# A weight sum of the attention branch worked out ahead and fetched, and one more seven-product quad in its first pass

## The chip, the cores and the metric

The kernel runs on one core of one Trainium2 chip. The metric is the device time of one execution in microseconds (us). Three runs of the kernel before gave a median of 1379.91 us (1379.5 to 1380.3).

## The reference, cut to what matters

One layer of a hybrid block on 256 rows of width 2048: a normalised input is projected (`proj`), one part goes through dilated attention, one through a state-space scan, and both come back through a gated sum:

```python
proj = hn @ w_in
q, k, v, z_a, z_s, xbc, dt_raw, g_a, g_s = jnp.split(proj, split_points, axis=-1)
...
o_a = o_a.reshape(b, s, ATTN_WIDTH) * jax.nn.silu(z_a)
...
merged = jax.nn.sigmoid(g_a) * (o_a @ w_attn_branch) + jax.nn.sigmoid(g_s) * (y @ w_ssm_branch)
return x + merged @ w_out
```

The change is about `o_a @ w_attn_branch`: 256 x 2048 times 2048 x 2048, in fp32.

## The kernel before, in words

**Products in three matmuls.** The matrix engine (PE) takes fp32r operands, so each fp32 operand is split into a high part (`h`, a copy by ACT) and a low part (`l = w - h`, a subtraction by DVE). A product is the triple h·h, h·l, l·h (`triple`, L484 to L486): three 128x512 matmuls. A PE instruction for `l` thus stands behind a DMA, an ACT copy and a DVE subtraction.

**Units, quads and passes.** Weights come as units of 128x1024 floats (512 KB) over SP's DMA queue, in an order laid out on the host. The GEMMs `ssm`, `v`, `ga`, `attn` and `out` run in two passes, c = 0 and c = 2, each of two column blocks of 512. A pass goes over its k in quads (two k-tiles, both row halves, both column blocks) in a written order (`A_ORDERS` for attn). A plain quad is 8 triples, 24 matmuls, and two units. A quad named in `S_QUADS` is done with seven products as in Strassen's method: 21 matmuls, for which it needs the weights A11 and A12 (tile `wa`, one unit), B22 (`wc`, half a unit), T (`wt`, one unit, a sum of weight blocks) and U = `wa` minus T's second half. On the side of the activations it needs `sx`, sums of activation blocks. In attn the first pass has the seven-product quads 2, 4, 6, the second 2, 4, 5, 6.

**Where T and U come from.** The sums T of ga, attn and out are worked out while the PE projects q, k and za (in the profile, some 825 to 1116 us): every 3.75 weight units a job of `sum_jobs` loads a unit and half a unit into `th_a` (L250, with a small POOL copy ahead that orders it behind unit u), three units later DVE makes T with two subtractions (L254, L255) and SP spills it to DRAM (L242). In the attn pass T is fetched into a place in `fin` (L533), B22 into another (L534), and U is made in place on DVE from `wa` (L565), at which point `la` has read `wa` already.

**Two banks of sums, a fold, two seams.** The seven products go to PSUM in two sets: `ps` tiles (results) and `pp` tiles (four products that several results share). At the end of a pass `fold` (L587 to L594) adds the four `pp` tiles up: two ACT copies, then DVE L591 (third `pp` tile), L592 (fourth), L593, L594; after that `ps` and fold are added (L1154) and merged with the gate (`merge`, L1143, L1144). In the first pass these run at the program's own priority, in the second ahead of it (`M_AHEAD`). Weight splits run 120 places ahead (`L_AHEAD`). Where one pass ends and the next begins (the seam), DVE has to serve both: the fold of the old pass and the low parts of the new one. All engines and the SP queue take their instructions in program order; that order is set by a scheduler from the written order and these priorities. Units are numbered through; 433 to 448 are those of attn's second pass (`l433` is the low part of its first unit, `ltt437` that of T of its first seven-product quad). `mtp` are 128x128 transposes on the PE of the merged rows (L1136).

Of the kernel before, what the change touches and what calls it, by code (L numbers as in the profile page):

```python
# [9 lines left out]
F32 = mybir.dt.float32  # L10
# [5 lines left out]
P = 128  # L16
# [8 lines left out]
UNIT = 1024  # L25
# [12 lines left out]
GT_LAGS = (3, 5, 6), (2, 3, 4)  # L38
Y_AFTER = 0, 0
GS_BEFORE = {0: (0, 1), 4: (2,)}  # L40
A_ORDERS = {0: (0, 1, 2, 4, 3, 6, 5, 7), 2: (0, 2, 1, 4, 3, 5, 6, 7)}
V_ORDERS = {0: (0, 2, 4, 1, 3, 5, 6, 7), 2: (0, 2, 1, 4, 3, 5, 6, 7)}
G_ORDERS = {c: (0, 2, 4, 1, 3, 5, 6, 7) for c in (0, 2)}
O_LEFT = {0: {0: (0, 3), 4: (1, 5)}, 2: {}}
# [5 lines left out]
S_QUADS = {  # L50
    ("ssm", 0): (5, 7, 8, 10, 11, 12, 13), ("ssm", 2): (3, 5, 7, 8, 10, 11, 12, 13),
    ("v", 0): (2, 3, 4, 5, 6), ("v", 2): (2, 4, 5, 6), ("ga", 0): (2, 3, 4, 5, 6), ("ga", 2): (2, 3, 4, 5, 6),
    ("attn", 0): (2, 4, 6), ("attn", 2): (2, 4, 5, 6), ("out", 0): (3, 5), ("out", 2): (3, 5),
}
Y_ORDERS = {0: (0, 1, 2, 3, 5, 4, 7, 8, 6, 10, 11, 9, 12, 14, 13, 15), 2: (0, 3, 1, 5, 2, 7, 8, 4, 10, 11, 6, 12, 9, 13, 14, 15)}
Y_LATE = {12: 4, 13: 6}
SX_Y = sorted({*S_QUADS[("ssm", 0)], *S_QUADS[("ssm", 2)]}, key=Y_ORDERS[0].index)
Y_SPARE = {q: int(q in S_QUADS[("ssm", 0)] and q in S_QUADS[("ssm", 2)]) for q in SX_Y}
SX_X = (2, 4, 3, 5, 6)
O_BEHIND = 3, 14, 15, 17  # L60
SUMS_ATT = [(t, q) for t in [(n, c) for n in ("ga", "attn", "out") for c in (0, 2)] for q in S_QUADS[t]]
ATT_QUADS = sorted({*S_QUADS[("attn", 0)], *S_QUADS[("attn", 2)]})
IN_PLACE = {"ssm": [(0, 12), (2, 12)]}
SUMS_SSM = [(t, q) for t in (("ssm", 0), ("ssm", 2), ("v", 0), ("v", 2)) for q in S_QUADS[t] if (t[1], q) not in IN_PLACE.get(t[0], ())]
# [134 lines left out]
def hybrid_block(ctx: ExitStack, tc: tile.TileContext, wall, xt, x, pk_d, cst_d, fw_d, out):  # L199
# [28 lines left out]

    loaded = {}
    on_unit = {}  # L230
    presum, lefts = {}, {}
    ssm_pool = []

    def behind_unit(n, f):
        on_unit.setdefault(n, []).append(f)
# [5 lines left out]
        kept[key] = dram.tile([P, *shape], F32, name=name, tag=name)  # L241
        nc.sync.dma_start(kept[key], src)  # L242

    def sum_jobs(jobs, units, places):

        def get(tag, q, t, b11, behind):
            n = FIRST[tag] + 2 * q
            for dst, src in ((t, wall[n + 1]), (b11, wall[n, :, :512])):
                gp.tensor_copy(dst[:, 0:1], behind)
                nc.sync.dma_start(dst, src)  # L250

        def add(tag, q, t, b11, res, behind):
            gp.tensor_copy(res[:, 0:1], behind)
            ve.tensor_tensor(res[:, :512], t[:, :512], b11, ALU.subtract)  # L254
            ve.tensor_tensor(res[:, 512:], t[:, 512:], res[:, :512], ALU.subtract)  # L255
            spill(presum, (tag, q), f"t_{tag[0]}{tag[1]}_{q}", res, [UNIT])

        for n, ((tag, q), u) in enumerate(zip(jobs, units)):
            t, b11, res = places[n % len(places)]
            behind_unit(u, lambda behind, a=(tag, q, t, b11): get(*a, behind))  # L260
            behind_unit(u + SUM_LAG, lambda behind, a=(tag, q, t, b11, res): add(*a, behind))

    def load(n, cuts=(0, UNIT)):
        if n not in loaded:
# [204 lines left out]
    def gemm_pair(tag, x_of, n_kt, sxs, swap, extra={}, close=1, order=None, room={}, tail=None):  # L469
# [22 lines left out]
        for at, q in enumerate(order):  # L492
            tick()
            for f in extra.get(q, ()):
                f()
            ks = [x_of(2 * q + k) for k in range(2)]
            a = [[(x[:, i * P : (i + 1) * P], x[:, S + i * P : S + (i + 1) * P]) for x in ks] for i in range(2)]
            n = first + 2 * q
            if q not in quads:
                ready = [] if at <= n_q - close else ready  # L500
                ready += [(a, k, *unit(n + k, (2, 512))) for k in range(2)]
                if n_q - close <= at < n_q - 1:
                    continue
                steps = [(e, i, c) for e in ready for i in range(2) for c in range(2)]
                if at == n_q - 1:
                    steps.sort(key=lambda s: s[1:])
                jobs = [(e, i, c, es[2 * i + c], WHOLE, at == 0 and e[1] == 0, e is ready[-1]) for e, i, c in steps]
                if tail and at == n_q - 1:
                    es.append(tail(prods))
                    _, i, c = steps[-1]  # L510
                    jobs = jobs[:-3]
                    for acc, cs in ((es[3][:, LEFT], LEFT), (es[4][:, LEFT], RIGHT)):
                        for n, e in enumerate(ready[-3:]):
                            jobs.append((e, i, c, acc, cs, cs is RIGHT and n == 0, n == 2))
                for (ae, k, h, l), i, c, acc, cs, start, stop in jobs:
                    triple(acc, *ae[i][k], h[:, c, cs], l[:, c, cs], start=start, stop=stop and at == n_q - 1)
                continue
            if not prods:
                prods = banks(p_tags, "pp")
            made = (tag, q) in presum  # L520

            def place(kind):
                if not room.get(kind):
                    t = ring(f"{kind}{n}")
                    return t[:, 512:] if kind == "wc" else t
                seats[kind] = seats.get(kind, -1) + 1
                return room[kind][seats[kind] % len(room[kind])]

            wa = ring(f"wa{n}")
            nc.sync.dma_start(wa, wall[n])  # L530
            if made:
                wt, wc = place("wt"), place("wc")
                nc.sync.dma_start(wt, presum[tag, q])  # L533
                nc.sync.dma_start(wc, wall[n + 1, :, 512:])  # L534
            else:
                wt = ring(f"wb{n}")
                wc = wt[:, 512:]
                nc.sync.dma_start(wt, wall[n + 1])

            def hl(where, suffix, tags, bufs):  # L540
                return [
                    where.tile([P, UNIT], F32R, name=f"{t}{suffix}{n}", tag=t, bufs=bufs) for t in tags
                ]

            def pair_of(suffix):
                sets = room.get("tl", ())
                seats["tl"] = (seats.get("tl", -1) + 1) % (2 + len(sets))
                return sets[seats["tl"] - 2] if seats["tl"] > 1 else hl(mul, suffix, ("ht", "lt"), 2)

            def part(src, h, l):  # L550
                ac.activation(h, src, AF.Copy)  # L551
                ve.tensor_tensor(l, src, h.bitcast(F32), ALU.subtract)  # L552

            two = lambda t: t.rearrange("p (k m) -> p k m", k=2)
            with tc.high_priority(L_AHEAD):
                if not made:
                    ve.tensor_tensor(wt[:, :512], wt[:, :512], wa[:, :512], ALU.subtract)
                ha, la = hl(stream, "a", "hl", H_BUFS)
                part(wa, ha, la)
                hc, lc = hl(stream, "c", "hl", H_BUFS)  # L560
                part(wc, hc[:, :512], lc[:, :512])
                if not made:
                    ve.tensor_tensor(wt[:, 512:], wt[:, 512:], wt[:, :512], ALU.subtract)
                t2 = wt[:, 512:].unsqueeze(1).to_broadcast([P, 2, 512])
                ve.tensor_tensor(two(wa), two(wa), t2, ALU.subtract)  # L565
                ht, lt = pair_of("t")
                part(wt, ht, lt)
                hu, lu = pair_of("u")
                part(wa, hu, lu)
            sx = sxs[q]  # L570
            lo, hi = slice(0, 512), slice(512, 1024)
            go, end = q == seven[0], q == seven[-1]
            for acc, x, h, l, cs, own in (
                (prods[0], a[0][0], ha, la, lo, True),
                (es[0], a[0][1], ha, la, hi, False),
                (es[1], sx[3], hc, lc, lo, False),
                (prods[1], sx[0], ht, lt, lo, True),
                (prods[2], sx[2], ht, lt, hi, True),
                (prods[3], sx[1], hu, lu, lo, True),
                (es[2], a[1][1], hu, lu, hi, False),  # L580
            ):
                triple(acc, *x, h[:, cs], l[:, cs], start=(own and go), stop=(own and end))
# [109 lines left out]
    with tc.tile_pool(name="ssm", bufs=2) as sp:  # L692
# [212 lines left out]
        for c in GS_BEFORE[0]:  # L905
# [4 lines left out]
        begin = FIRST[("xs", 4)]  # L910
        sum_jobs(
            SUMS_SSM, [FIRST[("B", g)] + n for g in range(1, 7) for n in SUM_UNITS],
            [(sums_at[:, 0], sums_at[:, 2, :512], sums_at[:, 1])],
        )

        def left_x(q, behind):
# [127 lines left out]
    with tc.tile_pool(name="att", bufs=2) as ap:  # L1044
# [33 lines left out]
        def mix(h, pT, za):  # L1078
# [10 lines left out]
            if h % 2 == 1 and q in ATT_QUADS:  # L1089
# [1 line left out]

        sum_jobs(
            SUMS_ATT, [FIRST[("q", 0)] + 3 + n * 15 // 4 for n in range(len(SUMS_ATT))],
            [
                (th_a[:, i, :UNIT], th_a[:, 1, UNIT + 512 * i : UNIT + 512 * i + 512], th_a[:, 0, UNIT:])
                for i in range(2)
            ],
        )

        for h in range(NH):  # L1100
# [23 lines left out]
            open_gate(c, es, prods)  # L1124
        tick(final=True)

    with tc.tile_pool(name="fin", bufs=2) as fp:
        fin = big.tile([P, 2, D], F32, name="fin", tag="yo1a")
        room = {"wt": [fin[:, i, UNIT:] for i in range(2)], "wc": [fin[:, i, :512] for i in range(2)]}

        def turn_m(c, pair, b):
            tp = bank(b, 4 if b == "g" else 2, f"mtp{c}{pair}")
# [26 lines left out]
        for n in range(4):  # L1159
            after(T_LAGS[n // 2], lambda a=(n // 2, n % 2, "g"): turn_m(*a))  # L1160
        attend(2)
        for n in range(4):
            after(M_LAG + 1 + n // 2, lambda a=(2 + n // 2, n % 2, ("m1", "m2")[n % 2]): turn_m(*a))
        for n in range(4):
# [118 lines left out]
```

## Time and profile before

| what | value |
|---|---|
| median of 3 runs | 1379.91 us (1379.5 to 1380.3) |
| profiled execution, its own time | 1379.87 us |
| its span, first to last instruction | 1378.0 us |
| around the span | 1.87 us |
| mean granted clock of the PE | 0.998 |

The profile is one execution. Busy time of an engine leaves out its waits; DMA share is the mean busy share of the core's 16 DMA engines, and GB/s is what they moved. On the profile's clock the stages are: up to 745 us the state-space branch, 745 to 825 v, 825 to 1116 q, k, za with the attention heads, 1116 to 1200 ga, 1200 to 1284 attn, then out.

### The profile page before, as it was taken

What the parts mean: (1) busy time and instruction counts of PE and PEld (TensorE: products, weight loads), DVE (VectorE), ACT (ScalarE), POOL (GpSimd) and SP (SyncE); (2) the same over time, 40 slices, a digit from 0 to 9 for tenths busy, and PEclk for the clock granted to TensorE, in tenths of its full rate; (3) what the DMA queues carried; (4) which work ended last, traced back from release to release, by engine and by line L of the source; (5) the groups of instructions that cost most, each with busy time, mean ns of one, the idle gap of its engine ahead of it and who ended that gap; (6) DMA issues with size and microseconds to landing.
All of it is one profiled execution on the core that took longest, in us unless ns stands there. A gap on an engine that the chain in (4) does not pass through costs nothing.

```text
span 1378.0 us, 20734 instructions
## 1 busy us (share of the span) xinstructions
PE 1366.8 (99%) x7260; PEld 1164.8 (85%) x7260; DVE 1177.0 (85%) x1763; ACT 840.0 (61%) x1310; POOL 161.7 (12%) x238
## 2 busy tenths in 40 slices
PE   9999999999999999999999999999999999999997
PEld 7888888888888888888888888888888888888886
DVE  6898899898899888788989888777877789988897
ACT  7655777675667676666565554454444557655564
POOL 2301211101020100010001001211211000400112
PEclk9999999999999999999999999999999999999999
DMA  9767878778787867578677568888889757875773
GB/s 342 237 190 237 298 267 286 262 244 288 248 277 237 298 203 220 174 242 277 228 261 270 211 215 316 306 275 280 306 298 302 230 163 267 291 244 173 246 273 122
DMA packets 106520, 348.15 MB, mean 253 GB/s; under 512 B 11888, under 2 KB 14256, under 8 KB 106416
## 3 DMA queue, kind: packets, MB, share of 16 engines
q1 hardware_dynamic: 104400, 340.67, 74.0%
q10 hardware_dynamic: 1440, 4.06, 0.8%
q0 software_dynamic: 576, 2.10, 0.4%
q8 instruction: 57, 0.93, 0.3%
q14 instruction: 47, 0.39, 0.1%
HBM read 316.97 MB, written 29.82 MB: 252 GB/s over the span
## 4 chain that ended last, share of the span: by engine, by line
PE 98%; DMA 0%; DVE 0%; ACT 0%; issue 0%; SPq 0%; POOL 0%; POOLq 0%; DVEq 0%
PE ps_xs L333 8%; PE ps_zs L333 8%; PE ps_k L333 4%; PE ps_za L333 4%; PE ps_q L333 4%; PE ps_zs L339 4%; PE ps_xs L339 4%; PE ps_ssm L485 3%; PE ps_ssm L486 3%; PE ps_ssm L484 3%; PE ps_q L339 2%; PE ps_za L339 2%; PE ps_k L339 2%; PE ps_gs L421 2%; PE ps_gs L422 2%; PE ps_gs L420 2%
## 5 line engine op out<-in xcount | busy, mean ns | idle before, releaser
L278 ACT ACTIVATE h<-w 128x1024 fp32r<-128x1024 f32 (+1 forms) x394 | 410.0, 1048 | 306.0 <-issue 73.7
L279 DVE TENSOR_TENSOR l<-w,h 128x1024 fp32r<-128x1024 f32 (+1 forms) x394 | 474.0, 1209 | 111.1 <-ACT h L278 106.9
L333 PE MATMUL ps_zs<-XT,h 128*128 128x512 f32 x496 | 172.0, 393 | 0.0
L333 PE MATMUL ps_xs<-XT,h 128*128 128x512 f32 x496 | 171.6, 393 | 0.0
L339 PE MATMUL ps_zs<-XT,l 128*128 128x256 f32 x496 | 134.6, 279 | 0.0
L339 PE MATMUL ps_xs<-XT,l 128*128 128x256 f32 x496 | 133.7, 277 | 0.0
L333 PEld LDWEIGHTS ps_xs<-XT,h 128*128 128x128 f32 x496 | 91.3, 188 | 19.4
L333 PEld LDWEIGHTS ps_zs<-XT,h 128*128 128x128 f32 x496 | 91.3, 188 | 18.9
L339 PEld LDWEIGHTS ps_zs<-XT,l 128*128 128x128 f32 x496 | 93.3, 188 | 2.1
L339 PEld LDWEIGHTS ps_xs<-XT,l 128*128 128x128 f32 x496 | 93.2, 188 | 2.1
L333 PE MATMUL ps_q<-XT,h 128*128 128x512 f32 x256 | 91.1, 404 | 0.0
L333 PE MATMUL ps_k<-XT,h 128*128 128x512 f32 x256 | 88.6, 395 | 0.0
L333 PE MATMUL ps_za<-XT,h 128*128 128x512 f32 x256 | 88.4, 394 | 0.0
L551 ACT ACTIVATE ha<-wa 128x1024 fp32r<-128x1024 f32 x45 | 47.5, 1056 | 45.9 <-PE ps_ssm L486 10.0
L339 PE MATMUL ps_q<-XT,l 128*128 128x256 f32 x256 | 68.4, 278 | 0.0
L339 PE MATMUL ps_k<-XT,l 128*128 128x256 f32 x256 | 68.4, 277 | 0.0
L339 PE MATMUL ps_za<-XT,l 128*128 128x256 f32 x256 | 68.4, 277 | 0.0
L552 DVE TENSOR_TENSOR la<-wa,ha 128x1024 fp32r<-128x1024 f32 x45 | 54.8, 1218 | 8.4 <-ACT ha L551 8.3
L552 DVE TENSOR_TENSOR ltu<-wa,htu 128x1024 fp32r<-128x1024 f32 x40 | 48.7, 1219 | 10.8 <-ACT htu L551 10.8
L793 ACT ACTIVATE gt<-acb,acT 128x128 f32<-128x128 f32 x128 | 44.1, 390 | 22.2 <-DMA acb<-acum_d 21.9
L333 PEld LDWEIGHTS ps_k<-XT,h 128*128 128x128 f32 x256 | 47.0, 188 | 9.9
L333 PEld LDWEIGHTS ps_q<-XT,h 128*128 128x128 f32 x256 | 47.1, 188 | 9.7
(691 smaller groups left out, 3347.8 us busy)
## 6 DMA issues: line engine op xcount, KB each, us to landing
w<-in_wall SPq DMA_DIRECT2D x390, 512.0 KB, 4.8
wa<-in_wall SPq DMA_DIRECT2D x45, 512.0 KB, 4.7
th_a<-in_wall SPq DMA_DIRECT2D x21, 512.0 KB, 4.7
sums_at<-in_wall SPq DMA_DIRECT2D x18, 512.0 KB, 5.0
acb<-acum_d SPq DMA_DIRECT2D x32, 256.0 KB, 3.8
t_ssm<-sums_at SPq DMA_DIRECT2D x13, 512.0 KB, 4.3
wt<-t_ssm SPq DMA_DIRECT2D x13, 512.0 KB, 4.7
th_a<-in_wall SPq DMA_DIRECT2D x21, 256.0 KB, 5.4
```

The source lines that it names most:

```text
L278: ac.activation(h[:, a:b], w[:, a:b], AF.Copy)
L279: ve.tensor_tensor(l[:, a:b], w[:, a:b], h[:, a:b].bitcast(F32), ALU.subtract)
L333: high = pe.matmul(acc, h[:, kk, :], xs_of(kt), start=(kt == 0), stop=False)
L339: low = pe.matmul(acc[:, S:], l[:, kk, :], xs_of(kt)[:, :S], start=False, stop=(kt == KT - 1))
L420: pe.matmul(accs[i], xh, h[:, kk], start=(kt == 0), stop=False)
L421: pe.matmul(accs[i], xh, l[:, kk], start=False, stop=False)
L484: pe.matmul(acc, xh, h, start=start, stop=False)
L485: pe.matmul(acc, xh, l, start=False, stop=False)
L486: pe.matmul(acc, xl, h, start=False, stop=stop)
L551: ac.activation(h, src, AF.Copy)
L552: ve.tensor_tensor(l, src, h.bitcast(F32), ALU.subtract)
L793: ac.activation(g4[:, n, b], acb[:, j, b // 2 * P : b // 2 * P + P], AF.Relu, scale=-1.0, bias=sc[:, h : h + 1],)
```

## The change

Three things change, all in the attention branch.

1. Quad 5 of attn's first pass becomes a seven-product quad (its `sx` is there already, the second pass uses it), and the order of the first pass becomes 0, 1, 2, 4, 5, 6, 3, 7, so four seven-product quads stand in a row and two plain quads at the end.
2. U of all eight seven-product quads of attn is worked out in `sum_jobs`, behind T. Such a job loads a whole unit in place of half a one, has one more DVE subtraction of 128x1024 (L264) and one more spill of 512 KB to DRAM. T's result goes to a tile of the pool `mul` (tag `lt`, two buffers) in place of a part of `th_a`. There are 22 jobs in place of 21.
3. In the attn passes U is fetched (L550) like T, into a new pool `branch` (tile `room_a`) with two places for U and two for B22, which no longer goes into `fin`. The DVE subtraction that made U in place (now L579) stays for the other GEMMs, and runs no more in attn.

```diff
-A_ORDERS = {0: (0, 1, 2, 4, 3, 6, 5, 7), 2: (0, 2, 1, 4, 3, 5, 6, 7)}
+A_ORDERS = {0: (0, 1, 2, 4, 5, 6, 3, 7), 2: (0, 2, 1, 4, 3, 5, 6, 7)}
...
-    ("attn", 0): (2, 4, 6), ("attn", 2): (2, 4, 5, 6), ("out", 0): (3, 5), ("out", 2): (3, 5),
+    ("attn", 0): (2, 4, 5, 6), ("attn", 2): (2, 4, 5, 6), ("out", 0): (3, 5), ("out", 2): (3, 5),
...
+U_QUADS = 2, 4, 5, 6
+SUMS_U = {(t, q) for t, q in SUMS_ATT if t[0] == "attn" and q in U_QUADS}
...
-            for dst, src in ((t, wall[n + 1]), (b11, wall[n, :, :512])):
+            b = b if (tag, q) in SUMS_U else b[:, :512]
+            for dst, src in ((t, wall[n + 1]), (b, wall[n, :, : b.shape[-1]])):
...
+            if (tag, q) in SUMS_U:
+                t2 = res[:, 512:].unsqueeze(1).to_broadcast([P, 2, 512])
+                two = b.rearrange("p (k m) -> p k m", k=2)
+                ve.tensor_tensor(two, two, t2, ALU.subtract)
+                spill(u_sums, (tag, q), f"u_{tag[0]}{tag[1]}_{q}", b, [UNIT])
...
+            if (tag, q) in u_sums:
+                wu = place("wu")
+                nc.sync.dma_start(wu, u_sums[tag, q])
...
-                t2 = wt[:, 512:].unsqueeze(1).to_broadcast([P, 2, 512])
-                ve.tensor_tensor(two(wa), two(wa), t2, ALU.subtract)
+                if (tag, q) not in u_sums:
+                    wu = wa
+                    t2 = wt[:, 512:].unsqueeze(1).to_broadcast([P, 2, 512])
+                    ve.tensor_tensor(two(wa), two(wa), t2, ALU.subtract)
...
-                part(wa, hu, lu)
+                part(wu, hu, lu)
...
-        room = {"wt": [fin[:, i, UNIT:] for i in range(2)], "wc": [fin[:, i, :512] for i in range(2)]}
+        spots = bp.tile([P, 3 * UNIT], F32, name="room_a", tag="room_a")
+        room = {
+            "wt": [fin[:, i, UNIT:] for i in range(2)],
+            "wu": [spots[:, i * UNIT : (i + 1) * UNIT] for i in range(2)],
+            "wc": [spots[:, 2 * UNIT + i * 512 : 2 * UNIT + i * 512 + 512] for i in range(2)],
+        }
```

How the order of instructions moves is shown at two places. Names carry a running number at their end; a name such as `pp_attn0_2` is the third `pp` tile of the first pass, `ps_attn2_0` the first result tile of the second. Lines of the kernel after are its own: L288 is L279 of before, L493 to L495 are L484 to L486, L564 is L552, L605 to L608 are L591 to L594, L1160, L1161 and L1171 are L1143, L1144 and L1154, L1153 is L1136.

**The seam between the two attn passes, on DVE.** Before, from the first fold step on:

```order
L591 TENSOR_TENSOR fin_12298<-pp_attn0_2_12380,fin_12298 128x512
L279 TENSOR_TENSOR l432_12589<-w432_12586,h432_12588 128x1024
L552 TENSOR_TENSOR ltt437_12721<-fin_12298,htt437_12720 128x1024
L592 TENSOR_TENSOR fin_12298<-pp_attn0_3_12381,fin_12298 128x512
L593 TENSOR_TENSOR fin_12298<-fin_12298 128x512
L279 TENSOR_TENSOR l433_12670<-w433_12667,h433_12669 128x1024
L594 TENSOR_TENSOR fin_12298<-fin_12298 128x512
L279 TENSOR_TENSOR l434_12676<-w434_12673,h434_12675 128x1024
L1154 TENSOR_TENSOR fin_12298<-ps_attn0_0_12299,fin_12298 128x512
```

And in the changed kernel, from the same step on:

```order
L605 TENSOR_TENSOR fin_12353<-pp_attn0_2_12436,fin_12353 128x512
L1171 TENSOR_TENSOR fin_12353<-ps_attn0_0_12355,fin_12353 128x512
L564 TENSOR_TENSOR ltt437_12783<-fin_12353,htt437_12782 128x1024
L1160 SCALAR_TENSOR_TENSOR th_a_7802<-th_a_7802,fin_12353 128x512
L606 TENSOR_TENSOR fin_12353<-pp_attn0_3_12437,fin_12353 128x512
L1161 SCALAR_TENSOR_TENSOR th_s_90<-th_a_7802,th_s_90 128x512
L607 TENSOR_TENSOR fin_12353<-fin_12353 128x512
L564 TENSOR_TENSOR ltu437_12787<-room_a_12354,htu437_12786 128x1024
L608 TENSOR_TENSOR fin_12353<-fin_12353 128x512
L1171 TENSOR_TENSOR fin_12353<-ps_attn0_1_12356,fin_12353 128x512
L288 TENSOR_TENSOR l433_12732<-w433_12729,h433_12731 128x1024
L288 TENSOR_TENSOR l434_12738<-w434_12735,h434_12737 128x1024
```

Before, five instructions stand between the first fold step's start and `l433`; in the changed kernel ten do (L605 counted in both cases).

**The same seam on PE.** Before, the second pass begins with `h433`, and `l433` is its second matmul:

```order
L486 MATMUL ps_attn0_3_12302<-h432_12588,oaTb_10585 128x512
L484 MATMUL ps_attn2_0_12635<-h433_12669,oaTa_8484 128x512
L485 MATMUL ps_attn2_0_12635<-l433_12670,oaTa_8484 128x512
L486 MATMUL ps_attn2_0_12635<-h433_12669,oaTa_8484 128x512
L484 MATMUL ps_attn2_1_12636<-h433_12669,oaTa_8484 128x512
```

In the changed kernel, first the last matmul into the third `pp` tile, then, 26 matmuls on, the seam:

```order
L495 MATMUL pp_attn0_2_12436<-htt429_12577,sx_o6_12371 128x512
...
L495 MATMUL ps_attn0_2_12357<-h432_12650,oaTb_10619 128x512
L1153 MATMUL mtp00_12701<-cst_77,th_s_90 128x128
L493 MATMUL ps_attn2_0_12697<-h433_12731,oaTa_8484 128x512
L493 MATMUL ps_attn2_1_12698<-h433_12731,oaTa_8484 128x512
L493 MATMUL ps_attn2_2_12699<-h433_12731,oaTa_8484 128x512
L493 MATMUL ps_attn2_3_12700<-h433_12731,oaTa_8484 128x512
L1153 MATMUL mtp01_12708<-cst_77,th_s_90 128x128
L494 MATMUL ps_attn2_0_12697<-l433_12732,oaTa_8484 128x512
```

Between the last matmul into `pp_attn0_2` and the first with `l433` stand 31 matmuls of 128x512 and two transposes. Two transposes of the first pass's rows (`mtp00`, `mtp01`) now stand ahead of `l433`; their PSUM banks are those of `ps_attn0_0` and `ps_attn0_1`, which L1171 has to have read.

**The SP queue in the second pass of ga.** Here the attn branch's first fetches stand among the loads of ga's weights. Before:

```order
L533 DMA fin_12298<-t_attn0_2_9856 128x1024
L534 DMA fin_12298<-in_wall 128x512
L533 DMA fin_12298<-t_attn0_4_9965 128x1024
L534 DMA fin_12298<-in_wall 128x512
L267 DMA w404_12076<-in_wall 128x1024
L533 DMA th_a_7802<-t_ga2_3_9358 128x1024
L530 DMA wa407_12109<-in_wall 128x1024
```

In the changed kernel:

```order
L542 DMA fin_12353<-t_attn0_2_9867 128x1024
L542 DMA fin_12353<-t_attn0_4_9980 128x1024
L276 DMA w404_12131<-in_wall 128x1024
L542 DMA th_a_7802<-t_ga2_3_9365 128x1024
L543 DMA room_a_12354<-in_wall 128x512
L550 DMA room_a_12354<-u_attn0_2_9870 128x1024
L543 DMA room_a_12354<-in_wall 128x512
L550 DMA room_a_12354<-u_attn0_4_9983 128x1024
L539 DMA wa407_12164<-in_wall 128x1024
```

Two fetches of U (512 KB each) now stand ahead of `wa407`, which is a weight of ga. On PE the first matmul with `ha407` moves back by 24 places (from row 5769 to row 5793 of the same sequence).

## Rows read from the trace of the kernel before

**Rows 1.** The page: the span, and busy time of each engine.
```profile
span 1378.0 us, 20734 instructions
PE 1366.8 (99%) x7260; PEld 1164.8 (85%) x7260; DVE 1177.0 (85%) x1763; ACT 840.0 (61%) x1310; POOL 161.7 (12%) x238
```

**Rows 2.** The page: the chain that ended last, shares by engine.
```profile
PE 98%; DMA 0%; DVE 0%; ACT 0%; issue 0%; SPq 0%; POOL 0%; POOLq 0%; DVEq 0%
```

**Rows 3.** The waits of PE, whole span: us in total, times, longest.
```profile
PE warm L630 <- DVE ssq L627: 1.4, 1, 1.4
PE ps_first L385 <- ACT h L278: 1.4, 2, 1.1
```

**Rows 4.** By stage: busy PE, PEld, DVE, ACT, POOL; granted clock, DMA share, GB/s.
```profile
825.00:1116.00 291.00, 291.00 (x1699) 255.70 (x1698) 220.65 (x420) 143.66 (x221) 43.57 (x63) 1.00 0.83 281
1116.00:1200.00 84.00, 83.98 (x376) 69.07 (x374) 77.97 (x96) 56.02 (x69) 14.72 (x8) 1.00 0.77 256
1200.00:1284.00 84.00, 84.00 (x380) 69.61 (x379) 75.21 (x87) 48.90 (x60) 3.16 (x1) 1.00 0.66 217
```

**Rows 5.** Timeline of PE in attn: start, duration, line, operation.
```profile
1222.89 0.39 PE L484 MATMUL ps_attn<-ha,oaTb 128*128 128x512 f32 x1
...
1232.41 0.39 PE L484 MATMUL ps_attn<-h,oaTb 128*128 128x512 f32 x1
```

**Rows 6.** Timeline of PE: six transposes and the matmul behind them.
```profile
1247.16 0.82 PE L1136 MATMUL mtp<-cst,th_s 128*128 128x128 f32 x6
1247.73 0.48 PE L484 MATMUL ps_attn<-hc,sx_o 128*128 128x512 f32 x1
```

**Rows 7.** DVE's subtraction that makes U, in the attn stretch.
```profile
L565 DVE TENSOR_TENSOR wa<-wa,fin x7: 1214/1217/1218, 1208.1 to 1273.7; 128x1024 f32<-128x1024 f32 x7
```

**Rows 8.** Timelines of PE and DVE: a fold's last matmul and first step.
```profile
1196.14 0.39 PE L486 MATMUL pp_ga<-htt,sx_x 128*128 128x512 f32 x1
1196.64 0.69 DVE L591 TENSOR_TENSOR th_a<-pp_ga,th_a 128x512 f32<-128x512 f32 x1 [0.24 <-PE pp_ga L486]
```

**Rows 9.** Timeline of DVE at the seam of the attn passes.
```profile
1231.63 1.22 DVE L552 TENSOR_TENSOR ltt<-fin,htt 128x1024 fp32r<-128x1024 f32 x1
1232.77 0.68 DVE L592 TENSOR_TENSOR fin<-pp_attn,fin 128x512 f32<-128x512 f32 x1
...
1234.38 1.23 DVE L279 TENSOR_TENSOR l<-w,h 128x1024 fp32r<-128x1024 f32 x1 [0.21 <-ACT h L278]
...
1237.57 1.28 DVE L1154 TENSOR_TENSOR fin<-ps_attn,fin 128x512 f32<-128x512 f32 x2
1238.77 1.28 DVE L1143 SCALAR_TENSOR_TENSOR th_a<-th_a,fin 128x512 f32<-128x512 f32 x2
1239.97 0.68 DVE L1154 TENSOR_TENSOR fin<-ps_attn,fin 128x512 f32<-128x512 f32 x1
```

**Rows 10.** Timeline of PE: the first matmul with the low part of unit 433.
```profile
1240.80 0.39 PE L485 MATMUL ps_attn<-l,oaTa 128*128 128x512 f32 x1
```

**Rows 11.** Timelines of SP, ACT and PE in ga: unit 407.
```profile
1168.55 0.33 SPq L530 DMA_DIRECT2D wa<-in_wall  x1
1172.87 1.06 ACT L551 ACTIVATE ha<-wa 128x1024 fp32r<-128x1024 f32 x1 [1.65 <-DMA wa<-in_wall]
1174.38 0.39 PE L484 MATMUL pp_ga<-ha,XT 128*128 128x512 f32 x1
```

**Rows 12.** Three stretches of the q, k, za stage, columns as in rows 4.
```profile
840.30:850.60 10.30, 10.30 (x62) 9.01 (x61) 7.54 (x11) 4.03 (x6) 0.87 (x3) 1.00 0.96 360
994.80:1005.10 10.30, 10.30 (x61) 9.03 (x60) 7.05 (x15) 4.42 (x6) 2.75 (x3) 1.00 0.96 336
1056.60:1066.90 10.30, 10.30 (x63) 9.11 (x62) 6.92 (x14) 4.45 (x7) 0.31 (x1) 1.00 1.01 373
```

**Rows 13.** Timelines of DVE and PE there: a low part, its first use.
```profile
1000.99 1.23 DVE L279 TENSOR_TENSOR l<-w,h 128x1024 fp32r<-128x1024 f32 x1 [1.55 <-ACT h L278]
1009.96 0.27 PE L339 MATMUL ps_q<-XT,l 128*128 128x256 f32 x1
```

More of the change, by code (lines that the diff above doesn't have):

```diff
@@ L230, in hybrid_block @@
     on_unit = {}
-    presum, lefts = {}, {}
+    presum, u_sums, lefts = {}, {}, {}
     ssm_pool = []
@@ L242, in spill, with sum_jobs, get, add @@
         nc.sync.dma_start(kept[key], src)
-    def sum_jobs(jobs, units, places):
-        def get(tag, q, t, b11, behind):
+    def sum_jobs(jobs, units, places, res):
+        def get(tag, q, t, b, behind):
             n = FIRST[tag] + 2 * q
-            for dst, src in ((t, wall[n + 1]), (b11, wall[n, :, :512])):
+            b = b if (tag, q) in SUMS_U else b[:, :512]
+            for dst, src in ((t, wall[n + 1]), (b, wall[n, :, : b.shape[-1]])):
                 gp.tensor_copy(dst[:, 0:1], behind)
                 nc.sync.dma_start(dst, src)
-        def add(tag, q, t, b11, res, behind):
+        def add(tag, q, t, b, res, behind):
+            res = res(f"t_{tag[0]}{tag[1]}_{q}")
             gp.tensor_copy(res[:, 0:1], behind)
-            ve.tensor_tensor(res[:, :512], t[:, :512], b11, ALU.subtract)
+            ve.tensor_tensor(res[:, :512], t[:, :512], b[:, :512], ALU.subtract)
             ve.tensor_tensor(res[:, 512:], t[:, 512:], res[:, :512], ALU.subtract)
             spill(presum, (tag, q), f"t_{tag[0]}{tag[1]}_{q}", res, [UNIT])
+            if (tag, q) in SUMS_U:
[3 more added lines that the diff above has]
+                spill(u_sums, (tag, q), f"u_{tag[0]}{tag[1]}_{q}", b, [UNIT])
         for n, ((tag, q), u) in enumerate(zip(jobs, units)):
-            t, b11, res = places[n % len(places)]
-            behind_unit(u, lambda behind, a=(tag, q, t, b11): get(*a, behind))
-            behind_unit(u + SUM_LAG, lambda behind, a=(tag, q, t, b11, res): add(*a, behind))
+            t, b = places[n % len(places)]
+            behind_unit(u, lambda behind, a=(tag, q, t, b): get(*a, behind))
+            behind_unit(u + SUM_LAG, lambda behind, a=(tag, q, t, b, res): add(*a, behind))
     def load(n, cuts=(0, UNIT)):
@@ L912, in hybrid_block @@
             SUMS_SSM, [FIRST[("B", g)] + n for g in range(1, 7) for n in SUM_UNITS],
-            [(sums_at[:, 0], sums_at[:, 2, :512], sums_at[:, 1])],
+            [(sums_at[:, 0], sums_at[:, 2, :512])], lambda name: sums_at[:, 1],
         )
@@ L1093, in hybrid_block @@
             SUMS_ATT, [FIRST[("q", 0)] + 3 + n * 15 // 4 for n in range(len(SUMS_ATT))],
[L1094 to L1097, printed above, removed]
+            [(th_a[:, i, :UNIT], th_a[:, i, UNIT:]) for i in range(2)],
+            lambda name: mul.tile([P, UNIT], F32, name=name, tag="lt", bufs=2),
         )
@@ L1125, in hybrid_block @@
         tick(final=True)
-    with tc.tile_pool(name="fin", bufs=2) as fp:
+    with tc.tile_pool(name="branch", bufs=1) as bp:
         fin = big.tile([P, 2, D], F32, name="fin", tag="yo1a")
-        room = {"wt": [fin[:, i, UNIT:] for i in range(2)], "wc": [fin[:, i, :512] for i in range(2)]}
+        spots = bp.tile([P, 3 * UNIT], F32, name="room_a", tag="room_a")
[4 more added lines that the diff above has]
+        }
         def turn_m(c, pair, b):
@@ L1161, in hybrid_block @@
         attend(2)
+    with tc.tile_pool(name="fin", bufs=2) as fp:
         for n in range(4):
```

## The prediction

> **What bounds the kernel now.** I read the page first. The span is 1378.0 us and the PE is busy in 1366.8 of them, 99%, DVE 85%, ACT 61% [rows 1]; the chain that ended last is PE work in 98% of the span [rows 2]. Busy time alone doesn't prove that PE is never kept waiting, so next came its waits: two in the whole span, 1.4 us each in total, both in the program's first microseconds (the warm-up and the first unit) [rows 3]. By stage, the attn stretch from 1200 to 1284 us has PE busy in 84.00 of 84.00, DVE in 75.21, and DMA at a share of 0.66 [rows 4]. So the end of the kernel is the number of matmuls times their distance. That distance is read from the timeline and not from a matmul's own 0.39 us, since matmuls overlap: from 1222.89 to 1232.41 there are 42 matmuls of 128x512, 9.52 / 42 = 0.2267 us each [rows 5]. Two things follow. What the change takes off DVE, ACT or DMA is worth nothing by itself. And every instruction that it makes late for PE is a loss, as PE has no slack to take it back.
>
> **The change, part by part.** The sum is made against the profiled execution, 1379.87 us, its span and 1.87 us around it; it stands 0.04 us under the median 1379.91.
>
> *Fourth seven-product quad.* 21 matmuls take the place of 24: 3 x 0.2267 = 0.68 us less [rows 5]. This is on the path, and it is all that can be won: −0.68.
>
> *U no more made in place.* Seven DVE subtractions of 1.22 us leave attn [rows 7], some 8.5 us of its 75.21 busy. PE waited for none of them [rows 3, 4], so they pay 0. What they give is room for the scheduler to place other DVE work earlier, which is the next part.
>
> *The seam between the attn passes.* This is the loss that I expect. Before, `l433` and `l434` went between the fold's steps: `l433` ran from 1234.38 to 1235.61 and its first matmul is at 1240.80, 5.2 us to spare [rows 9, 10]. In the changed order ten DVE instructions stand from the first fold step to `l433`, and the first of them can't begin before the last matmul into the third `pp` tile. I count both ways from that matmul's start.
> PE: itself and 31 matmuls, 32 x 0.2267 = 7.25 us, and two transposes at (1247.73 − 1247.16) / 6 = 0.095 us [rows 6], 0.19. PE would come to `l433` after 7.44 us.
> DVE: 0.50 us from the last matmul's start to the fold's first step, 1196.14 to 1196.64 [rows 8] (I take 0.45, since DVE's own wait there came out of an idle stretch and the step needs only the matmul's end). Eight steps of 128x512 at 0.60 (four of them from 1237.57 to 1239.97), two of 128x1024 at 1.14 (1231.63 to 1232.77), and `l433` itself to its end, 1.23 [rows 9]: 0.45 + 4.80 + 2.28 + 1.23 = 8.76 us.
> PE waits 8.76 − 7.44 = 1.3 us, most of it at `l433`, a first part of it at `mtp01`, whose bank is read by the step just ahead. Behind `l433` on PE's queue stands everything, so the end moves by that. From below: the scheduled distances may leave no stall if DVE starts the fold's first step at once and PE comes late, 0; from above: two of the ten may each lose 0.3 us to the ACT copies that they read (`htt437` waits for its buffer until the very matmul from which I count, `htu437` for one 15 matmuls later), 1.9. I take 1.3, as each of its terms is a row. After it DVE is ahead again: `l434` ends 1.14 us behind `l433`, and PE takes its 12 matmuls on unit 433, 2.7 us, before it needs it. In the seam from attn to out the new order has some two steps more ahead of the first low part, and I count about 2 us to spare there: 0.
>
> *Sums in the q, k, za stage.* Eight jobs load 256 KB more, spill 512 KB more and have one DVE step of 1.22 us (as in [rows 7]) more; one job is new. DVE is busy 220.65 of 291 there [rows 4], and PE takes units 7.7 us after their low parts are written: 1002.22 to 1009.96 [rows 13]. DVE's 9.8 us spread over 91 us are hidden by that. SP's queue is passed by eight more spills, each waiting for its DVE step; those steps stand ahead of the low parts for which the next loads wait, so they hold nothing back that isn't held already. DMA is the question. 96 units in 291 us are 3.03 us a unit [rows 4], a job's 3.75 units 11.4 us. Before, it moved 1.97 MB of weights, 0.79 of loads and 0.52 of spill, 3.28 MB or 288 GB/s; in the changed kernel 1.97 + 1.05 + 1.05 = 4.06 MB, 357 GB/s, for eight jobs, 91 us. The stage has moved 373 GB/s at a share of 1.01 and 336 at 0.96 [rows 12]. At 373 it keeps up; at 336 it falls behind by 91 x (357/336 − 1) = 5.7 us. So the bounds are 0 and, of those 5.7, whatever exceeds the 7.7 us that are there, which is 0 for an even backlog and perhaps 2 us if it comes where the margin is thin. I take 0.
> The Trainium skill ("DMA: Bandwidth & Descriptors", "Where 436 GB/s comes from") says that for transfers from HBM the limit of a core is about 358 GB/s, and the fabric's 435 binds others. It speaks against this change: with one spill of activations in the 91 us (0.52 MB, 6 GB/s) the stage asks 363, and by 358 as a strict limit, an estimate from that page, that is a backlog of 1.3 us, which the margin still hides; the sum stays, but the DMA rival below would get 0.25 and not 0.18. The rows show 373 for 10 us, so the limit isn't strict here, and I go by the rows.
>
> *Fetches in ga and attn.* Two fetches of U, 1.05 MB, now stand ahead of ga's unit 407. At the 373 GB/s of [rows 12] that is 2.8 us. Unit 407 was already the tightest place: issued at 1168.55, its ACT copy waited for the DMA until 1172.87 and ended 0.45 us before its first matmul at 1174.38 [rows 11]. A late copy would stop PE at once. But the matmul itself moves back by 24 places, 24 x 0.2267 = 5.4 us, so 0.45 + 5.4 − 2.8 = 3 us are left: 0. In attn the fetches of U and the new quad add some 4.4 MB to 84 x 217 = 18.2 MB, which makes 269 GB/s, below the 281 of the q, k, za stage [rows 4], where PE never waits. Each of the four sevens in a row wants 1.84 MB in 21 x 0.2267 = 4.8 us, 385 GB/s, more than any stretch of [rows 12], but T, B22 and U of the first two are fetched in ga already. Bounds 0 and 2, taken as 0.
>
> The sum: 1379.87 − 0.68 + 1.3 = 1380.5 us. This is 0.05% over the time before, within 0.2% (2.76 us), which is what a measurement of this kernel can tell from no change.
>
> **The rivals.**
> *No stall at the seam, 1379.2.* PE stays dense and the three matmuls are all that shows: 1379.87 − 0.68. For it speaks that PE waits nowhere now [rows 3]; against it the count above, which would have to be off by 1.3 us in 8.8. Chance 0.22.
> *DMA falls behind, 1382 to 1386: slower.* In the q, k, za stage the eight jobs ask 357 GB/s, and SP's queue is one: a load that is late makes every later one late. From the point where the backlog passes the 7.7 us of [rows 13], PE waits for what is beyond. If the stage can't do more than the 336 GB/s of [rows 12] and the other spills of the stage (0.5 MB each) fall into the same 91 us, the backlog is 5.7 us plus 0.5/0.336 = 1.6 us for each, and with two or three of these it passes the margin by 1 to 3 us; together with the seam that is 1381.5 to 1383.5, and a backlog that meets unit 407 in ga or the row of sevens in attn adds 1 to 2 more. Against it: the stretches of 336 and 360 GB/s have a share of 0.96, which leaves it open whether they were full. Chance 0.18, of which 0.11 beyond 0.2%.
> *The fold is the longer chain, faster than I think.* The whole of DVE's work in attn shrinks by 8.5 us; if PE had hidden waits there, they would go. The stretch has 84.00 of 84.00 busy [rows 4], so there is at most some tenths of a microsecond. Chance of a gain over 0.2%: 0.01.
> *The change doesn't do what it says.* The order of the changed kernel has three matmuls fewer, and no U step in attn. I see no way for it.
>
> **How the numbers follow.** The forecast with its stall between 0.8 and 1.9 (1380.0 to 1381.1) has 0.55, no stall 0.22, DMA behind 0.18, and 0.05 is left for a wait that I don't see, of which 0.01 is the gain and 0.02 over 0.2% slower. The range goes down to the dense case with 0.1 for the scatter of the three runs (0.4 either way), 1379.0, and up through the lesser half of the DMA case, 1382.8. Faster by over 0.2%: 0.01; slower: 0.11 + 0.02 = 0.13; within: 0.86.
>
> **What would show it.** PE's matmul count falls by three, and its waits get a third row: `l` or `mtp` from DVE at the seam, near 1241 us, of about 1.3 us in all, with ten DVE steps between the last matmul into the third `pp` tile and `l433`. DVE's busy time in attn falls by about 8 us less what the new quad brings, and nothing comes of it. DMA's share in the q, k, za stage rises above its 0.83, in the 91 us of the eight jobs to near 1, and low parts there are written later but still ahead of PE. Unit 407's first matmul is not waited for. I am wrong if PE waits for `h` or `l` in the q, k, za stage, if PE waits in ga, or if no wait shows at the seam.

## The result, and the profile after

The changed kernel takes 1385.37 us (median of 8 runs, 1382.99 to 1386.49); the kernel before, run beside it, 1380.38 us (8 runs, 1379.5 to 1381.03). The ratio is 1.0034, with a 95% interval of 1.0024 to 1.0045: slower by 5 us. The forecast was 1380.5 with a range of 1379.0 to 1382.8. The profiled execution took 1383.91 us, a short one among the eight.

The page's first lines, which answer to [rows 1]:

```profile
span 1382.1 us, 20822 instructions
PE 1367.7 (99%) x7257; PEld 1164.5 (84%) x7257; DVE 1180.4 (85%) x1768; ACT 841.8 (61%) x1312; POOL 166.0 (12%) x241
```

PE has its three matmuls fewer (7257 for 7260), and the busy shares say nothing of what went wrong. The waits of PE do (us in total, times, longest; [rows 3] before):

```profile
PE ps_out L495 <- DVE mT L297: 2.7, 1, 2.7
PE warm L644 <- DVE ssq L641: 1.4, 1, 1.4
PE ps_first L394 <- ACT h L287: 1.2, 1, 1.2
PE ps_attn L494 <- DVE l L288: 0.8, 1, 0.8
PE mtp L1153 <- DVE fin L1171: 0.2, 1, 0.2
```

The last two rows are the wait at the seam of the attn passes that was forecast. The first row is new, and the largest: a low part of the merged rows (`mT`, L297), some 20 us into the stage out, in code that the diff doesn't touch. The stages (columns as in [rows 4]):

```profile
825.00:1116.00 291.00, 291.00 (x1697) 255.64 (x1696) 229.44 (x429) 143.60 (x221) 55.10 (x66) 1.00 0.87 307
1116.00:1200.00 84.00, 83.89 (x375) 68.60 (x374) 77.69 (x97) 55.51 (x69) 8.93 (x8) 1.00 0.78 259
1200.00:1284.00 84.00, 82.98 (x373) 68.33 (x372) 69.30 (x83) 51.30 (x61) 0.21 (x1) 1.00 0.80 277
```

In the q, k, za stage the sums cost nothing: more DMA (0.87 for 0.83) and DVE (229 for 221), and PE busy throughout. In attn DVE has 5.9 us less to do, which buys nothing, and PE loses 1.0.

The seam, in the timelines of PE and DVE:

```profile
1234.22 0.39 PE L495 MATMUL pp_attn<-htt,sx_o 128*128 128x512 f32 x1
...
1234.65 0.69 DVE L605 TENSOR_TENSOR fin<-pp_attn,fin 128x512 f32<-128x512 f32 x1 [1.31 <-PE pp_attn L495]
...
1241.25 0.68 DVE L1171 TENSOR_TENSOR fin<-ps_attn,fin 128x512 f32<-128x512 f32 x1
1241.85 2.35 DVE L288 TENSOR_TENSOR l<-w,h 128x1024 fp32r<-128x1024 f32 x2
...
1241.99 0.33 PE L1153 MATMUL mtp<-cst,th_s 128*128 128x128 f32 x1 [0.22 <-DVE fin L1171]
1243.12 0.50 PE L494 MATMUL ps_attn<-l,oaTa 128*128 128x512 f32 x1 [0.80 <-DVE l L288]
```

From the last matmul into the third `pp` tile to the first with the low part of unit 433: 8.90 us, where PE alone needs 7.44. The stall is 1.46.

The wait in out, first PE, then DVE:

```profile
1304.53 0.39 PE L494 MATMUL ps_out<-l,mT 128*128 128x512 f32 x1
1307.67 1.19 PE L495 MATMUL ps_out<-h,mT 128*128 128x512 f32 x4 [2.75 <-DVE mT L297]
...
1301.45 1.22 DVE L564 TENSOR_TENSOR la<-wa,ha 128x1024 fp32r<-128x1024 f32 x1
1305.79 1.23 DVE L579 TENSOR_TENSOR wa<-wa,room_o 128x1024 f32<-128x1024 f32 x1 [3.12 <-DMA room_o<-t_out]
1306.93 1.28 DVE L297 TENSOR_TENSOR mT<-mtp,mT 128x512 fp32r<-128x512 f32 x2
```

DVE stands idle for 3.12 us in front of L579, the U of out's first seven-product quad, until T has come from DRAM, and the low parts of the merged rows, for which PE waits, stand behind it. The same place in the kernel before:

```profile
1299.34 1.22 DVE L552 TENSOR_TENSOR la<-wa,ha 128x1024 fp32r<-128x1024 f32 x1
1301.21 0.69 DVE L288 TENSOR_TENSOR mT<-mtp,mT 128x512 fp32r<-128x512 f32 x1 [0.66 <-ACT mT L286]
1303.77 1.22 DVE L565 TENSOR_TENSOR wa<-wa,room_o 128x1024 f32<-128x1024 f32 x1 [1.87 <-DMA room_o<-t_out]
1304.92 1.28 DVE L288 TENSOR_TENSOR mT<-mtp,mT 128x512 fp32r<-128x512 f32 x2
```

There DVE waits for the same fetch (1.87 us), but the first low part, the only one that PE needs soon, is done before that. The scheduler has put these two the other way round:

```diff
-L288 TENSOR_TENSOR mT<-mtp20 128x2x256
 L579 TENSOR_TENSOR wa455<-wa455,room_o 128x1024
+L297 TENSOR_TENSOR mT<-mtp20 128x2x256
 L297 TENSOR_TENSOR mT<-mtp21 128x2x256
```

The chain of the changed kernel at this place (start, us, what):

```profile
1291.79 4.61 POOL fin L659
...
1296.42 0.33 ACTq L660
...
1296.88 1.07 ACT h L287
...
1299.11 1.30 DVE th_s L1161 x2
...
1300.43 5.26 DMA room_o<-t_out
...
1305.79 1.23 DVE wa L579
1307.01 0.61 DVE mT L297
```

The fetch can't be issued before the last merge steps (L1161): its place `room_o` has the memory of `th_a`, which they read. Then it takes 5.26 us, to 1305.69. PE wanted the low part at 1304.76 (1304.53 and one matmul), so it waits for the end of the fetch, for U and for the low part itself.

Further up the chain stands POOL's copy of a single column (L659, 128x1): 4.61 us here, 0.18 us for the same copy in the kernel before. ACT's queue stands 5.15 us behind it and DVE 1.63 us behind ACT, ahead of the merge steps. Set against PE's need, the fetch ends 0.5 us later than before: L579 begins 2.02 us later than L565 did, PE's need comes 1.54 us later (1304.76 for 1303.22). That the copy is what costs this half microsecond is likely and not shown; why it takes longer isn't known.

The profiled execution adds up: 1379.87 − 0.68 (three matmuls) + 1.46 (seam) + 2.91 (1304.53 to 1307.67, less one matmul) + 0.25 (a wait for `htu` in ga, 1149.04 to 1149.52 where 0.23 would do) = 1383.8, against 1383.91 measured. The sum holds to some tenths and no closer: in the profile of the changed kernel the first matmul of v already stands 0.5 us later than in that of before (744.7 for 744.2), ahead of all that was changed. It leaves open why the median is 1.5 us higher still and the runs lie 3.5 us apart, those of before 1.5.

### The profile page after: what moved, and what is told of

Its sections match the earlier page's. It is cut to its first block, busy times and chain, and to the rows that moved or that the text cites. A ratio compares the mean times of both kernels' runs of the same rounds, so it can differ in the third digit from the quotient of the medians.

```text
span 1382.1 us, 20822 instructions
## 1 busy us (share of the span) xinstructions
PE 1367.7 (99%) x7257; PEld 1164.5 (84%) x7257; DVE 1180.4 (85%) x1768; ACT 841.8 (61%) x1312; POOL 166.0 (12%) x241
## 4 chain that ended last, share of the span: by engine, by line
PE 96%; DMA 1%; DVE 1%; issue 1%; ACT 0%; POOL 0%; SPq 0%; POOLq 0%; ACTq 0%; DVEq 0%
PE ps_xs L342 8%; PE ps_zs L342 8%; PE ps_za L342 4%; PE ps_k L342 4%; PE ps_q L342 4%; PE ps_zs L348 4%; PE ps_xs L348 4%; PE ps_ssm L494 3%; PE ps_ssm L495 3%; PE ps_ssm L493 3%; PE ps_q L348 2%; PE ps_k L348 2%; PE ps_za L348 2%; PE ps_gs L430 2%; PE ps_gs L431 2%; PE ps_gs L429 2%
## 5 line engine op out<-in xcount | busy, mean ns | idle before, releaser
L288 DVE TENSOR_TENSOR l<-w,h 128x1024 fp32r<-128x1024 f32 (+1 forms) x392 | 471.6, 1209 | 107.6 <-ACT h L287 103.3
L564 DVE TENSOR_TENSOR la<-wa,ha 128x1024 fp32r<-128x1024 f32 x46 | 56.1, 1219 | 11.6 <-ACT ha L563 10.7
L342 PEld LDWEIGHTS ps_za<-XT,h 128*128 128x128 f32 x256 | 46.9, 188 | 9.8
```

The lines of the kernel that those rows point to most:

```text
L288: ve.tensor_tensor(l[:, a:b], w[:, a:b], h[:, a:b].bitcast(F32), ALU.subtract)
L342: high = pe.matmul(acc, h[:, kk, :], xs_of(kt), start=(kt == 0), stop=False)
```

## The experiments

**Theory 1: order.** The loss is the two orders on DVE, above all L297 behind an instruction that waits for a DMA. **Theory 2, the rival: DMA.** The fuller queues make fetches late in several places, and the order hardly matters. All variants were timed in 5 rounds beside the kernel before: in the first four its median was 1380.51, in the others 1380.84. Where an order was changed, it was by a rule that issues one instruction behind another on the same engine, and adds no wait.

**The changed kernel again.** No edit.

> The changed kernel unaltered, for a second profile beside the variants. The first profile shows PE waiting 2.7 us in the out stage for a low part of the merged rows (DVE L297), which stands on DVE behind the subtraction that makes U of out's first seven-product quad (L579); that one waits 3.1 us for the fetch of T from DRAM. Theory 1 (order): this wait is the loss, and as it ends with the landing of a DMA, the time scatters; the profile will again show a wait at L495 behind L297, of 2 to 5 us, and a run as long as the wait is long: time about 1379.2 + 1.4 (seam) + 0.3 (ga) + the wait. Theory 2 (DMA): the loss comes from fuller DMA queues in more places, and the profile shows other waits of PE, in the q, k, za stage or ga, that the first one happened not to have. Time 1385.4 in either case, 0.36% over before.

Measured: 1385.22 us (1382.62 to 1386.96), ratio 1.0038 (1.0025 to 1.0050). The waits in the profile, taken of a run of 1385.10 us, are those of the first one; behind the program's start there is no other:

```profile
PE ps_out L495 <- DVE mT L297: 2.5, 1, 2.5
PE ps_attn L494 <- DVE l L288: 0.8, 1, 0.8
PE mtp L1153 <- DVE fin L1171: 0.2, 1, 0.2
```

The wait in out is no longer than in the first profile, yet the run is 1.2 us longer. Where that went is seen in two windows, the wait and the 3 us behind it (third column from the end: granted clock),

```profile
1304.60:1307.50 2.90, 0.42 (x2) 0.00 (x0) 1.87 (x3) 1.94 (x4) 0.00 (x0) 0.93 0.90 342
1307.50:1310.60 3.10, 3.09 (x7) 2.48 (x8) 3.10 (x5) 2.48 (x4) 0.00 (x0) 0.51 0.55 189
```

and in the timeline of PE from the first matmul behind the wait on:

```profile
1307.51 2.08 PE L495 MATMUL ps_out<-h,mT 128*128 128x512 f32 x4 [2.49 <-DVE mT L297]
...
1310.61 0.40 PE L493 MATMUL ps_out<-h,mT 128*128 128x512 f32 x1
```

Behind the wait the granted clock is at 0.51, its lower level of 1.2 GHz: 7 matmuls take 3.10 us where 7 x 0.2267 = 1.59 would do. That is 1.5 us more. In the first profile the clock stayed at 1.00 behind the same wait:

```profile
1307.70:1310.70 3.00, 3.00 (x13) 2.50 (x14) 3.00 (x5) 2.46 (x4) 0.36 (x1) 1.00 0.45 154
```

**The first low part of the merged rows put back ahead of U.**

```diff
...
+    turned = []
...
-            split(tp.rearrange("p (k s) -> p k s", k=2), mT[:, ks, :S], mT[:, ks, S:])
+            turned.append(split(tp.rearrange("p (k s) -> p k s", k=2), mT[:, ks, :S], mT[:, ks, S:]))
...
+                    with tc.issue_after(turned[4].ins) if (tag, q) == (("out", 0), 3) else nullcontext():
-                    ve.tensor_tensor(two(wa), two(wa), t2, ALU.subtract)
+                        ve.tensor_tensor(two(wa), two(wa), t2, ALU.subtract)
```

> The changed kernel with one order put back: L579 of out's first seven-product quad is issued behind the first L297 of the second pass's merged rows, as in the kernel before. Theory 1 (order): PE no longer waits for L297; what is left is the seam (1.4) and some tenths, 1381 to 1382, about 3.5 us under the changed kernel, and the runs lie within 1.5 us of one another as those of before do. Theory 2 (DMA): T lands late in any case, PE waits for its low part or for U a few matmuls on; 1384 to 1385.5, with the scatter of the changed kernel.

Measured: 1381.26 us (1379.84 to 1382.66), ratio 1.0008 (0.9999 to 1.0017): 4 us of the 5 are gone. The timeline of DVE:

```profile
1302.79 0.69 DVE L297 TENSOR_TENSOR mT<-mtp,mT 128x512 fp32r<-128x512 f32 x1
1305.22 1.23 DVE L581 TENSOR_TENSOR wa<-wa,room_o 128x1024 f32<-128x1024 f32 x1 [1.74 <-DMA room_o<-t_out]
```

And what is left of PE's waits behind the start:

```profile
PE ps_attn L495 <- DVE l L288: 0.8, 1, 0.8
PE mtp L1155 <- DVE fin L1173: 0.2, 1, 0.2
PE pp_ga L494 <- ACT htu L564: 0.2, 1, 0.2
```

DVE still waits for T until 1305.2. The fetch is issued no earlier than in the changed kernel (1300.46 for 1300.43) and lands 0.6 us earlier, behind PE's need of 1304.8, and PE no longer cares. Theory 1 holds; theory 2, by which PE would have waited for T a few matmuls on, falls. The scatter, which I had also named as a mark, tells little: of the 27 runs of the kernel before beside this variant 26 lie between 1379.22 and 1382.28 (one, of 3374.1 us, stands alone).

**At the seam, the low part of U of quad 437 behind those of units 433 and 434.**

```diff
...
-                part(wu, hu, lu)
+                with tc.issue_after(lows[FIRST[tag] + 1].ins) if (tag, q) == (("attn", 2), 2) else nullcontext():
+                    part(wu, hu, lu)
```

> The changed kernel with the low part of U of quad 437 (1.14 us of DVE) issued behind the low parts of units 433 and 434. By the count of the prediction the DVE chain from the third pp tile to the low part of 433 falls from 8.8 to 7.6 us against PE's 7.4: the wait at the seam falls from 1.4 to 0.2 or 0.3. If the wait in out stands by itself and moves with everything ahead of it, the time falls by 1.1, to 1384.2; if the fetch that ends it is held by something that doesn't move, the wait there grows by what is won here, and the time stays at 1385.4.

Measured: 1384.29 us (1380.52 to 1386.52), ratio 1.0028 (1.0018 to 1.0037), 0.9 under the changed kernel beside it, which the intervals can't tell from none. The profile says more: the wait in out is still there with 2.4 and no longer than before, so what lies ahead of it moves it along. At the seam, though, two waits of 0.3 us stand in the list for one of 0.8, the second at the low part of unit 435: DVE has no idle time between the two, and what is put behind the one is ahead of the other.

**Both orders.** The two edits together.

> Both orders put back. If the two waits are the whole loss, what is left is the three matmuls (-0.7), some 0.3 at the seam and 0.3 in ga: 1380.3, the same as before within 0.05%, with before's scatter. If a third cause costs in most runs, it stays over 1382.

Measured: 1380.53 us (1379.35 to 1382.24), ratio 1.0001 (0.9992 to 1.0010). The loss is these two places; no third cause is left that can be measured, which here means over some 1.2 us.

**The cause put into the kernel before.** Its L288 of the merged rows is issued behind its L565, nothing else.

```diff
...
-                ve.tensor_tensor(two(wa), two(wa), t2, ALU.subtract)
+                u = ve.tensor_tensor(two(wa), two(wa), t2, ALU.subtract)
+                if (tag, q) == (("out", 0), 3):
+                    tc.add_manual_dep(turned[4].ins, u.ins.name, ...)
```

> The kernel before, with one order changed: the first L288 of the second pass's merged rows stands behind L565 of out's first seven-product quad, as in the changed kernel; no more DMA, no fourth quad, no U ahead. If that order is the cause, PE waits for L288 here too: L565 began at 1303.77 in the profile of before and the low part would end 1.8 us later, against a use near 1303.0, so a wait of 2.5 us, and, as in the second profile of the changed kernel, matmuls at half the clock for some 3 us behind it in a part of the runs, 1.6 us more: 1383 to 1384.5, with a scatter of 3 us. If the cause is the fuller DMA of the change, nothing happens: 1380.5.

Measured: 1383.43 us (1382.31 to 1385.28), ratio 1.0022 (1.0013 to 1.0030). With the DMA traffic and the attn branch of before, PE's wait:

```profile
PE ps_out L487 <- DVE mT L288: 2.3, 1, 2.3
```

and on DVE:

```profile
1304.62 1.23 DVE L566 TENSOR_TENSOR wa<-wa,room_o 128x1024 f32<-128x1024 f32 x1 [3.25 <-DMA room_o<-t_out]
```

One exchange of two instructions makes the kernel before slower by 2.6 us.

**The fourth quad without U ahead.**

```diff
-U_QUADS = 2, 4, 5, 6
+U_QUADS = ()
```

> The changed kernel without U ahead: the fourth seven-product quad and its order stay, U is made in place by DVE. Three matmuls fewer as in the change. By the count of instructions DVE reaches the low part of unit 433 5.8 us behind the third pp tile, PE 6.6, and the merged rows' low parts stand ahead of L579: no wait at either place, 1379.8, 0.05% under before, with its scatter. If the fourth quad needs U ahead to be fed (the rival: DVE with eight U steps more in attn becomes late), PE waits in attn for a U or a low part and the time is over 1381.

Measured: 1384.23 us (1383.26 to 1385.22), ratio 1.0026 (1.0017 to 1.0036). My count of this variant was wrong, and the rival's time and its waits in attn came true. The two places that I had looked at are without a wait; five other rows stand in the list:

```profile
PE ps_attn L494 <- DVE l L288: 1.2, 2, 0.7
PE pp_ga L493 <- ACT ha L563: 1.0, 1, 1.0
PE ps_out L493 <- ACT fin L603: 0.7, 1, 0.7
PE ps_attn L494 <- DVE ltu L564: 0.3, 1, 0.3
PE pp_ga L493 <- ACT htu L563: 0.2, 1, 0.2
```

and on ACT in ga:

```profile
1176.13 1.06 ACT L563 ACTIVATE ha<-wa 128x1024 fp32r<-128x1024 f32 x1 [3.34 <-DMA wa<-in_wall]
```

With eight U steps of 1.2 us in attn, DVE is late for low parts in the second pass: 1.5 us of the waits (L288 and `ltu`) are there. The other 1.9 us are not the rival's: a weight of ga that comes late by DMA (the place of [rows 11]), `htu` in ga, and a copy of the fold by ACT that PE waits for at its first matmuls of out. What brings those wasn't tested. So in this order the fourth quad doesn't pay without U ahead; that the U steps are the whole reason isn't shown.

**U ahead without the fourth quad.** `A_ORDERS` and `S_QUADS` of attn as before.

> The change without its fourth quad: order and quads of the first attn pass as before, U summed ahead and fetched for the seven that remain. The matmuls are those of before. Both seams have the order of before (merged rows ahead of L579, low part of unit 433 with 59 matmuls' time behind the third pp tile). If DMA is hidden, as I now think: 1380.5, no change. If the 7 spills and 7 wider loads of the q, k, za stage or the fetches cost by themselves, 1381 or more, and the profile shows PE waiting there.

Measured: 1380.89 us (1380.38 to 1382.82), ratio 1.0002 (0.9994 to 1.0011). PE waits nowhere behind its start, with 300 GB/s in the q, k, za stage and 265 in attn:

```profile
825.00:1116.00 291.00, 291.00 (x1699) 255.69 (x1698) 227.81 (x427) 143.94 (x221) 53.60 (x63) 1.00 0.86 300
1200.00:1284.00 84.00, 84.00 (x381) 69.66 (x380) 67.89 (x81) 48.82 (x59) 4.71 (x1) 1.00 0.78 265
```

The DMA and DVE traffic of these seven sums is hidden, and the relief of DVE in attn by 7.3 us is worth nothing.

**Fourth quad and U ahead, first pass in the order of before, merged rows' low part ahead.**

```diff
-A_ORDERS = {0: (0, 1, 2, 4, 5, 6, 3, 7), 2: (0, 2, 1, 4, 3, 5, 6, 7)}
+A_ORDERS = {0: (0, 1, 2, 4, 3, 6, 5, 7), 2: (0, 2, 1, 4, 3, 5, 6, 7)}
```

and the edit on `turned` above.

> Fourth quad and U ahead both, but with the first pass in the order of before (0, 1, 2, 4, 3, 6, 5, 7) and the merged rows' first low part ahead of L579. The low part of unit 433 then stands ahead of the whole fold. If order is all that cost, only the three matmuls and the tenths in ga are left: 1380.0, 0.03% under before. This is the version that the first four runs point to.

Measured: 1380.07 us (1379.19 to 1382.81), ratio 0.9997 (0.9987 to 1.0006). The seam's wait is gone with the old order of quads. The median is the lowest of all, but 0.03% can't be told from no change, and the 0.05% that three matmuls are could not either.

## Why the prediction was wrong

**What bounds the kernel: right.** Only PE's instructions and its waits counted; DVE's relief was worth 0.

**Three matmuls: right,** 7257 for 7260, and with both orders put back only two waits of 0.3 us at the seam are seen to stand against them. No median is clear enough of noise to show their 0.68 us by itself.

**The seam between the attn passes: right in place, kind and size.** 1.3 us was forecast at `mtp01` and `l433`; 1.46 is what the timeline gives, as the chain took 8.90 us for the 8.76 counted.

**The seam from attn to out: the step that failed.** "In the seam from attn to out the new order has some two steps more ahead of the first low part, and I count about 2 us to spare there: 0." The count was of the first low part of a weight unit, and there PE doesn't wait indeed. But the same stretch of DVE's order holds the low parts of the merged rows and a U step that waits for DRAM, and these two changed places. The term was 2.9 us in the first profile, and 1.5 more in the second, in which the clock fell behind it. The order of the changed kernel shows the exchange, and the trace of before shows the 1.87 us that DVE waits for that fetch; put side by side, they give most of the loss: behind L565, the low part would have been done at 1304.92 + 0.69 = 1305.6 in the kernel before, against a need at 1303.2, so 2.4 us. I had compared the orders at the places that the diff speaks of. The exchange is none of the diff's own parts: neither the fourth quad alone nor U ahead alone has it in its profile, both together in the new order do.

**Sums and fetches: right, but for a quarter of a microsecond.** Neither the q, k, za stage nor unit 407 made PE wait, with all eight sums (first profile, 291.00 of 291.00 busy) or with seven (the variant with U ahead alone). In the first pass of ga PE lost 0.25 us at `htu`, which the sum had at 0; a wait in ga was one of the signs of being wrong, and it is a small one. The stage could do more than I took as its upper bound; a stretch of it in the changed kernel:

```profile
994.80:1005.10 10.30, 10.30 (x62) 8.98 (x61) 8.18 (x16) 4.67 (x6) 2.15 (x3) 1.00 1.02 408
```

The limit of about 358 GB/s from HBM that the Trainium skill ("DMA: Bandwidth & Descriptors", "Where 436 GB/s comes from") states was no ceiling for this core, which ran alone: the stretch moved 50 GB/s more for 10 us. By that rule I would have held the DMA rival likelier, and it was not the cause.

**The rivals.** Slower by over 0.2% had a chance of 0.13, nearly all of it on DMA in the q, k, za stage. The side was among the rivals, its mechanism was not: 0.02 was what I left for a wait that I don't see.

**What stays open.** How often the clock falls behind the wait isn't known: of four profiles with such a wait two show it (the one above, and the variant of the seam with 0.50), two don't. The mean granted clock on record for each run says that it is a part of the scatter. Where the cause was put into the kernel before, the four runs at 0.997 took 1384.23 to 1385.28 us and the seven at 0.998 or 0.999 took 1382.31 to 1383.88. In that variant, the one of the seam and the second set of runs of the changed kernel, 13 of 27 runs are at 0.997 or below; of the kernel before beside them no run is. In the eight runs of the result none is below 0.998, so that the clock is what puts their median 1.5 us above the profiled run isn't shown. Another part lies ahead of the change: in the ten profiles the first matmul of v starts between 743.9 and 745.0 us. A place of its own for out's T, so that its fetch needn't wait for the merge, was not tried.

## What to carry to other kernels

When a scheduler orders the work, a change can reorder code that it doesn't touch: go through the changed order of the whole stretch behind the edit, and mark first every instruction that waits for a DMA on an engine that PE depends on, since what slips behind it inherits that wait. An engine that idles in front of a fetch without harm is a warning; it is harmless only as long as nothing urgent is queued there. And where an engine is busy 99%, three instructions fewer are worth their own time and no more, while one exchange of two costs four times as much.

## What the runs showed of the hardware

A pause of PE can cost more than its length. Four profiles have a pause of PE in out, taken from the start of one matmul to that of the next, behind a stretch in which PE was busy throughout. Behind the one of 2.88 us (the changed kernel again) the granted clock was 0.51 for 3.1 us, with seven matmuls of 128x512 0.44 us apart for 0.23. Behind the one of 2.82 us (the variant of the seam) it was 0.50:

```profile
1306.40:1309.40 3.00, 3.00 (x7) 2.42 (x8) 3.00 (x5) 2.38 (x4) 0.00 (x0) 0.50 0.55 189
```

Behind the two others, of 3.14 us (the first profile) and 2.70 us (the cause put into the kernel before), it stayed at 1.00. So a pause of this length cost clock in two profiles and not in the two others, and which it will be isn't told by its length.
